# Modulation steps, context output rows and squares moved to other places in a diffusion layer's program

## The chip, the core and the metric

The kernel runs on one core of one Trainium2 chip. The metric is the device time of one execution in microseconds; the time before is the median of three runs. Inputs and outputs lie in the chip's memory (HBM).

## What is computed

The reference is one layer of a diffusion backbone: 1024 latent tokens and 256 context tokens, each 1024 wide, go through a half-step FFN, two token mixers side by side (a short gated convolution, and attention with grouped heads), a merge, and a second half-step FFN. All is float32.

```python
def rms_norm(x, g):
    y = x * lax.rsqrt(jnp.mean(x * x, axis=-1, keepdims=True) + EPS)
    return y * g
def modulate(h, shift, scale):
    return h * (1.0 + scale) + shift
def swiglu(h, w_in, w_out):            # w_in 1024 x 5632, w_out 2816 x 1024
    a, b = jnp.split(h @ w_in, 2, axis=-1)
    return (jax.nn.silu(a) * b) @ w_out
def short_conv(u, w): ...              # three taps along the tokens
def conv_branch(bg, cg, vc, conv_w):
    return bg * short_conv(cg * vc, conv_w)
def merge_branches(y_conv, o_attn, gate_logits, w_bc, w_ba, w_out):
    g_conv, g_attn = jnp.split(jax.nn.sigmoid(gate_logits), 2, axis=-1)
    return (g_conv * (y_conv @ w_bc) + g_attn * (o_attn @ w_ba)) @ w_out
```

Every sub-layer begins with such a norm and a modulation, and its result is added to the stream times a gate. The nine vectors of shift, scale and gate come from `silu(c) @ w_mod + b_mod` for the latent tokens and from `silu(c_ctx) @ w_mod + b_mod` for the context tokens; `w_mod` is 1024 x 9216.

## The kernel before

**Arithmetic.** A float32 product is made as three matmuls on rounded parts: `split` (line 187) casts a tile to its high part on ACT and subtracts it on DVE (now and then on POOL) for the low part; `mm3` takes high by high, high by low and low by high. A left operand's parts carry the names `wh` and `wl` (`wo` for output rows), a right operand's `r`, `rh`, `rl`.

**Winograd.** The large products over the 1024 latent tokens are taken as 2 x 2 blocks with seven products in place of eight (class `Winograd`). `lefts` loads weights (`raw`), forms sums of blocks on POOL (`s`), and hands out split left operands in a fixed order; `prefetch` draws them ahead; `product(i)` is 12 matmuls of 128 x 512 into one PSUM bank. Tiles `u`, `c`, `v`, `b`, `uc` hold the sums of the banks.

**The opening.** Tokens are transposed on PE, normed and split; meanwhile the first modulation vectors are made. `second_mod` (line 336) makes half a vector: DVE sums eight rows of `w_mod` times a scalar each (`macc<-rawm,silu_c`, one step each), then a split (`acch`, `accl`), two matmuls with a column of ones, a copy `mrow` on ACT, four transposes, and an addition into `modl`. It is a generator: `run(steps, n)` lets it advance by n steps, and where the program calls it decides where its instructions stand.

**The first FFN.** The loop over the 22 hidden blocks `j` makes each block's gate and value. From block `SIDE_FROM` = 12 on, the context tokens' product runs at the side of it, with the same weights (`side`, 48 matmuls of 128 x 256 and, at its end, `sa` and `hidc`, the hidden values of the context). After block 11 the twelve earlier blocks' sides are made by themselves, with the weights drawn again: this is called the context stage below. After every second block `context_out(j)` loads two rows of the output weights (`raw<-in_ffn_w_out_dram`), splits them (`wo`), and multiplies (`ps<-hidc,wo`, 48 matmuls), adding into `cacc`. `run(steps, STEPS[j])` advances the later modulation vectors (`later_mod`, line 262: loads of `rawm`, additions into `macc`, a product with ones, `mrow`, four small DMAs to `mcol`).

**The row products.** `row_products` (line 791) is the FFN's second matrix product, over the rows of the output weights and the hidden values read back from memory (`hid<-hd`), in the order i = 2, 1, 4, 6, 5, 7, 3 of the seven products, each in groups over pairs k of hidden blocks. `after1(i, k)` is called behind a group; it loads the stream `x` back, stores finished columns and makes their squares (`done`: `xd` stores, `sq` on ACT, `sq_acc` on DVE).

**The mixing.** `mix.start(norm1)` makes the first products of the next Winograd stage while the last right operands are normed; then a loop over eight blocks, `mixed`, makes the mixers' inputs, with `late_steps`, the last modulation vectors, run in it.

**What sets the order.** Each engine runs its instructions in its own order and waits on semaphores. Stretches of the program keep the order in which they are written; elsewhere a scheduler arranges it in the build. SP issues all DMAs of the main queue in order. Buffers come from rotating pools: 38 large tiles (`atile`), 11 tiles of 128 x 512 (`ttile`), three `raw` and four each of `wh` and `wl` for weights, and eight PSUM banks (five `ps`, two `pt`, one `po`). A load waits until the buffer that it writes is free.

All compute instructions are recorded at line 88, a wrapper round the engines, so the profile's groups are told apart by tile names.

```python
STEPS = (0, 4, 4, 4, 5, 5, 5, 5, 5, 5, 5, 14)
residual = {(2, 4): (C0, 0), (1, 6): (C0, 4), (4, 8): (C1, 0), (6, 4): (C1, 4)}
```

Of the kernel before, what the change touches and what calls it, by code (L numbers as in the profile page):

```python
# [10 lines left out]
F32R = mybir.dt.float32r  # L11
I32 = mybir.dt.int32
AF = mybir.ActivationFunctionType
ALU = mybir.AluOpType
# [27 lines left out]
STEPS = (0, 4, 4, 4, 5, 5, 5, 5, 5, 5, 5, 14)  # L42
# [7 lines left out]
def tile_dit_layer(  # L50
# [415 lines left out]
    class Winograd:  # L466
# [194 lines left out]
        def start(self, norm):  # L661

            for i in range(self.n_ahead):
# [3 lines left out]
                run(norm, 1)  # L667
# [123 lines left out]
    def row_products(w, rows, add, after=lambda i, k: None, halves=False):  # L791
# [113 lines left out]
        chain = [ps_t(), ps_t(), ps_o(), ps_s()]  # L905
        for i in (2, 1, 4, 6, 5, 7) + (() if halves else (3,)):
            ps = chain if i in (1, 6, 7) else [ps_s() for _ in range(4)]
# [99 lines left out]
    def left_operand(i, k):  # L1007
# [5 lines left out]
        else:  # L1013
            half1.shifted(h, c)
        half1.keep(1 + i, k, h)

# [39 lines left out]
    run(squares1, 1)  # L1056
    run(mod11, 3)
    run(start, 1)
    half1.prefetch(4, lo_engines=(pool, pool))
    run(squares1, 1)  # L1060
# [8 lines left out]
    run(mod11, 3)  # L1069
# [4 lines left out]
    run(mod11, 3)  # L1074
    run(start, 1)
    run(squares1)
    half1.prefetch(4)
    half1.rstd1 = token_rstd(ss1, 4)
    turned((4, 5))
    run(start, 1)  # L1080
    run(mod11)
    part_gain(gain1["l"], 0, "g1", "l", 4, 8)
    run(mod01, 9)
    half1.prefetch(4)
    turned((6, 7))
# [87 lines left out]
    def context_out(j):  # L1173

        ws = out_pieces(ffn1_w_out[0], (j - 1, j), spare=True)
        half1.prefetch(3)
        g = hid_c.pop(j // 2)
        for d in range(0, KD, 2):
            po = ps_s()
# [11 lines left out]

    for j in range(NH):
        half1.side = side(j) if j >= SIDE_FROM else None
        u, c = half1.next_first()
# [16 lines left out]
    for d in range(0, KD, 2):  # L1211
        t = ttile("cx")
        src = cxd[d // 4, :, (d % 4) * CT : (d % 4 + 2) * CT]
        sp.dma_start(out=t, in_=src)
        for e in range(2):
            te = t[:, e * CT : (e + 1) * CT]
            dve.scalar_tensor_tensor(
# [652 lines left out]
```

## Time and profile before

| | before |
|---|---|
| median of three runs | 2720.67 us (2720.63 to 2721.49) |
| the profiled execution | 2717.89 us, span 2716.1 us |
| mean granted clock of TensorE | 0.991 |
| PE busy in the span | 2647.6 us, 68.5 us idle |
| HBM read, written | 296.30 MB, 66.06 MB |

A row of the timeline gives start and length in microseconds, engine, line, operation, tiles written `<-` read, and in brackets the idle time of the engine ahead of it and what ended it. Rows of equal kind that follow one another are taken together (`x12`). A row of the windows gives the busy time of each engine in the stretch, the granted clock, the DMA engines' mean busy share and their rate. Times are counted from the span's start.

The opening lies at 0 to 110 us, the context stage at about 280 to 420, the row products of the first FFN from 693, the mixing's start at about 970.

### The profile page before, as it was taken

Reading aid. Unit: us, or ns where it says so; the run is one execution under the profiler, and the core shown is the slowest. Engines: PE = TensorE matmul, PEld = TensorE weight load, DVE = VectorE, ACT = ScalarE, POOL = GpSimd, SP = SyncE. Lnnn points to the kernel's source line nnn. Section 1 sums busy time; section 2 is a strip of 40 time slices with the busy share of each in tenths; the row PEclk is TensorE's granted clock in tenths of the full one; section 3 lists DMA queues with packets and bytes.
Section 4 is the critical chain, followed back from the end, with each engine's and each line's share of the span. In section 5 each row is a group of like instructions: output and inputs, shape, how many; then the busy total and the mean of one; then the engine's idle time right before and its main releaser. Section 6 shows DMA issues by size and latency. Waiting matters only on the chain.

```text
span 2716.1 us, 37388 instructions
## 1 busy us (share of the span) xinstructions
PE 2647.6 (97%) x13593; PEld 2236.8 (82%) x13593; DVE 2006.6 (74%) x3356; ACT 1167.2 (43%) x2317; POOL 532.1 (20%) x409
## 2 busy tenths in 40 slices
PE   7999899999999999999999999999999999999998
PEld 4788798888778877888999888877888888888888
DVE  5889666988787899888478576685548876667885
ACT  5633443333443542333245665674226333334443
POOL 1244001221010043333033111100000442330100
PEclk9999999999999999999999999999999999999998
DMA  7665553445984345433312321001533552227831
GB/s 264 212 195 170 166 168 100 147 129 179 324 206 105 113 151 186 135 118 120 109 32 87 97 82 43 28 32 47 175 105 124 179 163 93 86 89 283 183 86 63
DMA packets 369922, 364.85 MB, mean 134 GB/s; under 512 B 27831, under 2 KB 261449, under 8 KB 369737
## 3 DMA queue, kind: packets, MB, share of 16 engines
q1 hardware_dynamic: 360712, 345.17, 38.5%
q0 software_dynamic: 9024, 17.30, 4.0%
q8 instruction: 106, 1.74, 0.3%
q14 instruction: 80, 0.65, 0.1%
HBM read 296.30 MB, written 66.06 MB: 133 GB/s over the span
## 4 chain that ended last, share of the span: by engine, by line
PE 55%; DVE 3%; ACT 1%; issue 0%; DMA 0%; DVEq 0%; ACTq 0%
PE ps L88 45%; PE pt L88 5%; PE po L88 4%; DVE xb L88 0%; DVE ol L88 0%; ACT pts L88 0%; DVE pts L88 0%; DVE wl L88 0%; DVE x L88 0%; DVE r L88 0%; ACT pl L88 0%; DMA y<-yd 0%; ACT q L88 0%; ACT oh L88 0%; DVE t L88 0%
## 5 line engine op out<-in xcount | busy, mean ns | idle before, releaser
L88 PE MATMUL ps<-r,wl 128*128 128x512 f32 x5232 | 1208.9, 391 | 14.9 <-ACT wl L88 7.9
L88 PEld LDWEIGHTS ps<-r,wl 128*128 128x128 f32 x5232 | 979.8, 188 | 223.1 <-ACT wl L88 10.0
L88 ACT CAST wl<-raw 128x512 fp32r<-128x512 f32 x286 | 176.9, 620 | 291.2 <-PE ps L88 191.6
L88 POOL TENSOR_TENSOR s<-raw 128x512 f32<-128x512 f32 x64 | 95.5, 1492 | 1011.0 <-DMA raw<-in_ffn_w_in_dram 641.7
L88 ACT CAST wl<-s 128x512 fp32r<-128x512 f32 x256 | 158.0, 620 | 315.1 <-PE ps L88 233.4
L88 DVE TENSOR_TENSOR wl<-raw,wl 128x512 fp32r<-128x512 f32 x284 | 198.6, 700 | 80.8 <-ACT wl L88 77.0
L88 DVE TENSOR_TENSOR wl<-s,wl 128x512 fp32r<-128x512 f32 x256 | 230.3, 900 | 12.6 <-ACT wl L88 11.6
L88 POOL TENSOR_TENSOR s<-raw,s 128x512 f32<-128x512 f32 x64 | 107.3, 1677 | 355.2 <-DVE wl L88 347.3
L88 DVE SCALAR_TENSOR_TENSOR macc<-rawm,silu_c,macc 128x512 f32<-128x512 f32 x168 | 141.0, 855 | 8.5 <-DMA rawm<-in_w_mod_dram 7.4
L88 PE MATMUL ps<-wh,r 128*128 128x256 f32 x768 | 141.6, 285 | 0.0
L88 DVE TENSOR_TENSOR pts<-pt,pts 128x512 fp32r<-128x512 f32 x160 | 108.8, 687 | 39.3 <-ACT pts L88 38.3
L88 DVE TENSOR_REDUCE m<-ps 128x1 f32<-128x512 f32 (+1 forms) x192 | 110.9, 596 | 31.1 <-PE ps L88 30.3
L88 DVE TENSOR_TENSOR u<-u,ps 128x512 f32<-128x512 f32 x168 | 114.1, 679 | 23.2 <-PE ps L88 22.9
L88 ACT CAST pts<-pt 128x512 fp32r<-128x512 f32 x160 | 93.2, 593 | 88.6 <-PE pt L88 86.7
L88 PE MATMUL ps<-rh,wl 128*128 128x512 f32 x360 | 123.7, 395 | 3.9 <-ACT rh L88 3.9
L88 ACT CAST rh<-hid 128x512 fp32r<-128x512 f32 x132 | 81.0, 620 | 103.4 <-PE ps L88 86.3
L88 PEld LDWEIGHTS ps<-wh,r 128*128 128x128 f32 x768 | 120.6, 192 | 0.0
L88 ACT CAST wh<-raw 128x512 fp32r<-128x512 f32 (+1 forms) x88 | 69.4, 796 | 100.5 <-PE ps L88 73.0
L88 PE MATMUL po<-pts,vh 128*128 128x512 f32 x256 | 110.6, 438 | 1.5 <-ACT pts L88 1.5
L88 PE MATMUL ps<-wl,r 128*128 128x256 f32 x384 | 108.8, 283 | 0.0
L88 DVE TENSOR_TENSOR rl<-hid,rh 128x512 fp32r<-128x512 f32 x132 | 89.9, 686 | 23.8 <-ACT rh L88 11.4
L88 PE MATMUL ps<-kl,qs 128*128 128x512 f32 x384 | 105.3, 397 | 0.0
(295 smaller groups left out, 5082.0 us busy)
## 6 DMA issues: line engine op xcount, KB each, us to landing
raw<-in_ffn_w_in_dram SPq DMA_DIRECT2D x125, 512.0 KB
raw<-in_ffn_w_out_dram SPq DMA_DIRECT2D x72, 512.0 KB
rawm<-in_w_mod_dram SPq DMA_DIRECT2D x128, 256.0 KB
raw<-in_w_in_dram SPq DMA_DIRECT2D x61, 512.0 KB
hid<-hd SPq DMA_DIRECT2D x40, 512.0 KB
ws<-in_ffn_w_out_dram POOLq DMA_DIRECT2D x30, 512.0 KB, 6.6
ucd<-uc SPq DMA_DIRECT2D x22, 512.0 KB
hd<-c SPq DMA_DIRECT2D x38, 256.0 KB
```

Of the source, the lines that this page charges most:

```text
L88: inst = getattr(self.engine, name)(*args, **kw)
```

## The change

It has seven parts. In the opening, the steps of the two `second_mod` (`mod11` and `mod01`) and the token squares are called in other places, a few at a time; `mod11` begins with the first left operands. In the first FFN, `STEPS` becomes 2 at block 11 and 12 from block 12 on, and three steps are run at each of the context stage's twelve sides. `context_out` is cut into three: `context_rows` issues the row loads ahead of the pair's first side, `context_parts` splits them after it, and the product itself is made one pair late (`pending`, `context_last`); the last one, with the residual of the context, moves into the row products at (2, 0) and writes the `po` bank. `done(range(4), C0)` moves from (1, 11) to (4, 2). The four banks of the products 1, 6 and 7 are taken when i = 1 begins. `mix.start` advances its norm by 2, 1, 1, 1, 1, 3, ... in place of 1 each. The late modulation steps of the mixing are 5 + 4 + 4 in place of 13 at once.

```diff
-STEPS = (0, 4, 4, 4, 5, 5, 5, 5, 5, 5, 5, 14)
+STEPS = (0, 4, 4, 4, 5, 5, 5, 5, 5, 5, 5, 2, 12)
...
-                run(norm, 1)
+                run(norm, 2 if i == 0 else 1 if i < 5 else 3)
...
-        chain = [ps_t(), ps_t(), ps_o(), ps_s()]
+        chain = None
         for i in (2, 1, 4, 6, 5, 7) + (() if halves else (3,)):
+            if i == 1:
+                chain = [ps_t(), ps_t(), ps_o(), ps_s()]
...
-    def left_operand(i, k):
+    def left_operand(i, k, between=iter(())):
...
+        run(between, 1 - k % 2)
         half1.keep(1 + i, k, h)
+        run(between, 1 - k % 2)
...
+    mod11 = second_mod(1, 1, raws11)
     for k in range(4):
-        left_operand(0, k)
+        left_operand(0, k, mod11)
     start = half1.start_together()
-    mod11 = second_mod(1, 1, raws11)
     half1.prefetch(5, lo_engines=(pool, pool))
     for k, pt in banks.items():
         scaled(k, pt)
+    run(mod11, 2)
...
     turned((0, 1))
-    run(mod11, 3)
+    run(mod01, 3)
+    run(mod11, 1)
     run(start, 1)
     run(squares1, 1)
     half1.prefetch(4, lo_engines=(pool, pool))
     turned((2, 3))
-    run(mod11, 3)
+    run(mod11)
+    part_gain(gain1["l"], 0, "g1", "l", 4, 8)
+    run(mod01, 3)
...
+    turned((4, 5))
+    run(mod01, 3)
...
-    run(mod01, 9)
...
-    def context_out(j):
-
-        ws = out_pieces(ffn1_w_out[0], (j - 1, j), spare=True)
-        half1.prefetch(3)
+    def context_rows(j):
+        raws = []
+        for i in (j - 1, j):
+            t = atile("raw")
+            load(t[:], ffn1_w_out[0, i * P : (i + 1) * P, :])
+            raws.append(t)
+        return raws
+    def context_parts(j, raws):
+        ws = {}
+        for i, t in zip((j - 1, j), raws):
+            for half in range(2):
+                wt = wpool.tile([P, 2, 512], F32R, tag="wh", name=uniq("wo"), bufs=W_BUFS)
+                split(t[:, half * 512 : (half + 1) * 512], wt[:, 0], wt[:, 1])
+                ws[i, half] = wt
+        return ws
+    def context_out(j, ws, bank=ps_s):
         g = hid_c.pop(j // 2)
...
+    pending = []
+    def context_last(bank=ps_s):
+        if pending:
+            half1.prefetch(3)
+            context_out(*pending.pop(), bank)
     for j in range(NH):
         half1.side = side(j) if j >= SIDE_FROM else None
+        if j > SIDE_FROM and j % 2:
+            raws = context_rows(j)
...
             for i in range(SIDE_FROM):
+                if i % 2 == 0:
+                    raws = context_rows(i + 1)
                 do = side(i, ps_s)
                 for step in (1, 2, 0, 4):
                     do(step, half1.left())
-                if i % 2:
-                    context_out(i)
-        elif j >= SIDE_FROM and j % 2:
-            context_out(j)
+                run(steps, 3)
+                if i % 2 == 0:
+                    context_last()
+                    ws = context_parts(i + 1, raws)
+                else:
+                    pending.append((i, ws))
+        elif j > SIDE_FROM and j % 2:
+            pending.append((j, context_parts(j, raws)))
+        elif j >= SIDE_FROM:
+            context_last()
...
+    def context_residual():
+        context_last(ps_o)
+        for d in range(0, KD, 2):
...
+        if (i, k) == (2, 0):
+            context_residual()
+        if (i, k) == (4, 2):
+            done(range(4), C0)
         if k == NH // 2:
-            if i == 1:
-                done(range(4), C0)
-            elif i == 7:
+            if i == 7:
...
         if i > 1:
-            run(late_steps, 13)
+            run(late_steps, 5)
         for ch, bg, gc in mixed():
+            if i > 1:
+                run(late_steps, 4)
```

No engine has an instruction more or less; only places differ. Three of them follow in the built programs' order.

The first is DVE in the opening, before: `modl` is the addition that ends a modulation half, the eight `macc` rows sum the next half, `h` and `r` are the right operand that needs it.

```order
L88 TENSOR_TENSOR modl<-pt_510,bcol 128x4
L88 TENSOR_SCALAR gain_l<-modl 128x4
L88 TENSOR_TENSOR gain_l<-gain_l,cols 128x4
L88 TENSOR_SCALAR macc_518<-rawm_351,silu_c 128x512
L88 SCALAR_TENSOR_TENSOR macc_518<-rawm_351,silu_c,macc_518 128x512
L88 SCALAR_TENSOR_TENSOR macc_518<-rawm_353,silu_c,macc_518 128x512 x2
L88 SCALAR_TENSOR_TENSOR macc_518<-rawm_355,silu_c,macc_518 128x512 x2
L88 SCALAR_TENSOR_TENSOR macc_518<-rawm_357,silu_c,macc_518 128x512 x2
L88 TENSOR_TENSOR accl_528<-macc_518,acch_527 128x512
```

The same half in the changed program, on the same engine, stands as follows:

```order
L88 TENSOR_TENSOR accl_369<-macc_279,acch_368 128x512
L88 TENSOR_SCALAR macc_409<-rawm_358,silu_c 128x512
L88 SCALAR_TENSOR_TENSOR macc_409<-rawm_358,silu_c,macc_409 128x512
L88 SCALAR_TENSOR_TENSOR macc_409<-rawm_360,silu_c,macc_409 128x512
L88 TENSOR_TENSOR modl<-pt_451,bcol 128x4
L88 TENSOR_SCALAR gain_l<-modl 128x4
L88 TENSOR_TENSOR gain_l<-gain_l,cols 128x4
L88 SCALAR_TENSOR_TENSOR macc_409<-rawm_360,silu_c,macc_409 128x512
L88 SCALAR_TENSOR_TENSOR macc_409<-rawm_362,silu_c,macc_409 128x512 x2
L88 TENSOR_TENSOR wl_481<-raw_478,wl_481 128x512
L88 SCALAR_TENSOR_TENSOR macc_409<-rawm_364,silu_c,macc_409 128x512 x2
```

The second half's sums now begin ahead of the `modl` of the first, whose own sums lie among the lo parts of the first right operands.

The second place is SP's queue at the head of the context stage, before; `in_ffn_w_in` are loads of left weights, `in_ffn_w_out` the output rows of the first pair.

```order
L88 DMA raw_2667<-in_ffn_w_in_dram 128x8x128
L88 DMA raw_2807<-in_ffn_w_in_dram 128x8x128
L88 DMA raw_2809<-in_ffn_w_in_dram 128x8x128
L88 DMA raw_2878<-in_ffn_w_in_dram 128x8x128
L88 DMA raw_2719<-in_ffn_w_out_dram 128x1024
L88 DMA raw_2727<-in_ffn_w_out_dram 128x1024
```

In the changed program the first pair's rows stand in SP's queue so:

```order
L88 DMA raw_2482<-in_ffn_w_in_dram 128x8x128
L88 DMA raw_2550<-in_ffn_w_out_dram 128x1024
L88 DMA raw_2552<-in_ffn_w_out_dram 128x1024
L88 DMA rawm_2439<-in_w_mod_dram 128x512
L88 DMA raw_2570<-in_ffn_w_in_dram 128x8x128
```

The two rows are now ahead of modulation loads and of the left weights of the first sides. On PE, between the second pair's last side and the next side (`h1ch`, `h1cl`), before:

```order
L88 MATMUL ps_2948<-hidc_2856,wo_2934 128x256 x2
L88 MATMUL ps_2962<-hidc_2856,wo_2934 128x256 x2
L88 MATMUL ps_2976<-hidc_2856,wo_2937 128x256 x2
L88 MATMUL ps_2990<-hidc_2856,wo_2937 128x256 x2
L88 MATMUL ps_2948<-hidc_2856,wo_2934 128x256
L88 MATMUL ps_2962<-hidc_2856,wo_2934 128x256
L88 MATMUL ps_2976<-hidc_2856,wo_2937 128x256
L88 MATMUL ps_2990<-hidc_2856,wo_2937 128x256
L88 MATMUL ps_3004<-h1ch_1119,wl_2882 128x256
```

And on PE in the changed program, between two sides:

```order
L88 MATMUL ps_3023<-hidc_2796,wo_2864 128x256 x3
L88 MATMUL ps_3023<-hidc_2796,wo_2858 128x256 x3
L88 MATMUL ps_3023<-hidc_2796,wo_2864 128x256 x3
L88 MATMUL ps_3037<-hidc_2796,wo_2864 128x256 x3
L88 MATMUL ps_3037<-hidc_2796,wo_2858 128x256 x3
L88 MATMUL ps_3037<-hidc_2796,wo_2864 128x256 x3
L88 MATMUL ps_3051<-hidc_2796,wo_2867 128x256 x3
L88 MATMUL ps_3051<-hidc_2796,wo_2861 128x256 x3
L88 MATMUL ps_3051<-hidc_2796,wo_2867 128x256 x3
L88 MATMUL ps_3065<-hidc_2796,wo_2861 128x256 x3
L88 MATMUL ps_3065<-hidc_2796,wo_2867 128x256 x3
L88 MATMUL ps_3065<-hidc_2796,wo_2861 128x256 x3
```

Where 12 matmuls of the output product stood between two sides, 36 and more stand now, of the pair before.

The third place is DVE where the row products begin, before; `cacc` are the context's sums, `cx` its residual, `modl<-mcol` a late modulation vector, `rl` the lo parts of the rows:

```order
L88 TENSOR_TENSOR rl_6697<-hid_6636,rh_6696 128x512
L88 TENSOR_TENSOR rl_6718<-hid_6640,rh_6717 128x512
L88 TENSOR_TENSOR rl_6740<-hid_6640,rh_6739 128x512
L88 SCALAR_TENSOR_TENSOR cx_6614<-cacc_1123,gate_c,cx_6614 128x256 x2
L88 SCALAR_TENSOR_TENSOR cx_6619<-cacc_1123,gate_c,cx_6619 128x256 x2
L88 SCALAR_TENSOR_TENSOR cx_6624<-cacc_1124,gate_c,cx_6624 128x256 x2
L88 TENSOR_TENSOR rl_6761<-hid_6644,rh_6760 128x512
L88 TENSOR_TENSOR modl<-mcol_6532,bcol 128x4
```

And on DVE in the changed program, at the start of the row products:

```order
L88 TENSOR_TENSOR rl_6592<-hid_6560,rh_6591 128x512
L88 TENSOR_TENSOR cacc_1123<-cacc_1123,po_6632 128x512
L88 TENSOR_TENSOR u_6353<-u_6353,v_6413 128x512
L88 TENSOR_TENSOR rl_6617<-hid_6560,rh_6616 128x512
L88 TENSOR_TENSOR modl<-mcol_6536,bcol 128x4
L88 TENSOR_TENSOR cacc_1123<-cacc_1123,po_6646 128x512
L88 TENSOR_TENSOR wh_6613<-raw_6586,wh_6613 128x512
L88 SCALAR_TENSOR_TENSOR cx_6688<-cacc_1123,gate_c,cx_6688 128x256 x2
L88 TENSOR_TENSOR rl_6714<-hid_6564,rh_6713 128x512
L88 SCALAR_TENSOR_TENSOR cx_6693<-cacc_1123,gate_c,cx_6693 128x256 x2
```

The `modl` addition and the `cx` rows, which need DMAs, come ahead of the third `rl`, and the `cacc` additions are now in the row products.

More of the change, by code (lines that the diff above doesn't have):

```diff
@@ L1055, in tile_dit_layer @@
     squares1 = token_squares(t1, ss1)
-    run(squares1, 1)
     run(mod11, 3)
     run(start, 1)
+    run(squares1, 1)
     half1.prefetch(4, lo_engines=(pool, pool))
-    run(squares1, 1)
     def turned(ks):
@@ L1073, in tile_dit_layer @@
     turned((2, 3))
-    run(mod11, 3)
+    run(mod11)
+    part_gain(gain1["l"], 0, "g1", "l", 4, 8)
+    run(mod01, 3)
+    run(start, 1)
+    run(squares1, 1)
+    half1.prefetch(4)
+    turned((4, 5))
+    run(mod01, 3)
     run(start, 1)
@@ L1077, in tile_dit_layer @@
     half1.prefetch(4)
+    turned((6, 7))
+    run(mod01, 1)
     half1.rstd1 = token_rstd(ss1, 4)
[L1079 to L1082, printed above, removed]
-    run(mod01, 9)
-    half1.prefetch(4)
-    turned((6, 7))
     run(start, 1)
@@ L1171, in tile_dit_layer @@
     c_acc = Context("cacc")
-    def context_out(j):
-        ws = out_pieces(ffn1_w_out[0], (j - 1, j), spare=True)
-        half1.prefetch(3)
+    def context_rows(j):
[14 more added lines that the diff above has]
+    def context_out(j, ws, bank=ps_s):
         g = hid_c.pop(j // 2)
         for d in range(0, KD, 2):
-            po = ps_s()
+            po = bank()
             for e in range(2):
```

19 lines of the change are left out of this document (9 added, 10 removed).

## The prediction

> **What bounds the kernel now.** I read the page first, for the busy shares, the clock row and the costliest groups.
>
> ```profile
> span 2716.1 us, 37388 instructions
> PE 2647.6 (97%) x13593; PEld 2236.8 (82%) x13593; DVE 2006.6 (74%) x3356; ACT 1167.2 (43%) x2317; POOL 532.1 (20%) x409
> ...
> PEclk9999999999999999999999999999999999999998
> ...
> L88 DVE SCALAR_TENSOR_TENSOR macc<-rawm,silu_c,macc 128x512 f32<-128x512 f32 x168 | 141.0, 855 | 8.5 <-DMA rawm<-in_w_mod_dram 7.4
> ```
>
> The reader is to see that PE is busy for 2647.6 of 2716.1 us, so 68.5 us of idle time is all that a pure reordering can win, plus what the halved clock costs behind idle stretches. The change issues the same instructions on every engine (48 matmuls write another bank), so its whole price or gain is in PE's gaps. So I went next to the windows and the timeline of PE, at each place that the diff touches. First the windows (busy time of PE, PEld, DVE, ACT, POOL, then granted clock, DMA share and GB/s):
>
> ```profile
> 280.00:420.00 140.00, 122.71 (x936) 118.50 (x936) 90.28 (x144) 57.68 (x109) 9.14 (x6) 0.96 0.48 155
> 280.00:300.00 20.00, 14.12 (x104) 12.97 (x103) 19.56 (x32) 7.61 (x14) 0.00 (x0) 0.98 0.74 236
> 300.00:310.00 10.00, 5.80 (x28) 5.80 (x29) 4.84 (x10) 3.92 (x9) 0.00 (x0) 0.52 0.42 149
> 690.00:700.00 10.00, 8.46 (x38) 6.70 (x38) 5.69 (x10) 4.44 (x8) 0.00 (x0) 0.83 0.92 339
> 758.00:768.00 10.00, 6.79 (x23) 4.90 (x22) 9.90 (x17) 8.19 (x14) 1.21 (x1) 0.83 1.03 329
> 1074.00:1081.00 7.00, 3.99 (x10) 2.86 (x11) 6.79 (x12) 3.22 (x6) 2.73 (x2) 0.76 0.28 101
> 44.00:64.00 20.00, 14.09 (x74) 10.43 (x74) 14.06 (x32) 11.73 (x24) 1.31 (x1) 0.91 0.16 47
> ```
>
> The context stage, 280 to 420, alone holds 140 - 122.71 = 17.3 us of PE's idle time, a quarter of the whole. What ends those waits is the view of waits for PE in that window (total us, times, longest):
>
> ```profile
> PE ps L88 <- ACT wo L88: 10.1, 3, 9.0
> PE ps L88 <- DVE sa L88: 6.1, 5, 1.6
> PE ps L88 <- DVE wl L88: 1.1, 3, 0.6
> ```
>
> **The change part by part: the context stage.** The timelines of PE, ACT and SP's queue there:
>
> ```profile
> 304.20 2.08 PE L88 MATMUL ps<-hidc,wo 128*128 128x256 f32 x8 [8.98 <-ACT wo L88]
> 324.44 1.83 PE L88 MATMUL ps<-hidc,wo 128*128 128x256 f32 x12 [0.36 <-ACT wo L88]
> ```
> ```profile
> 303.53 2.37 ACT L88 CAST wo<-raw 128x512 fp32r<-128x512 f32 x4 [1.97 <-DMA raw<-in_ffn_w_out_dram]
> ```
> ```profile
> 290.86 7.96 SPq L88 DMA_DIRECT2D raw<-in_ffn_w_in_dram  x4
> 298.86 1.05 SPq L88 DMA_DIRECT2D raw<-in_ffn_w_out_dram  x2
> ```
>
> PE is still for 8.98 us because the cast of the first output rows starts at 303.53, when their DMA lands; and SP issues that DMA only at 298.86, behind four loads of weights for later left products that took it 7.96 us, each waiting for a buffer that DVE frees (DVE is busy for 19.56 of the 20 us before 300). In the changed order the two rows stand ahead of these loads and of the modulation rows, and their product is done one pair later, so three removals follow. The 8.98 us go. The halved clock behind them goes: 8 matmuls took 2.08 us at 304.20 where 12 take 1.83 at 324.44, and the window 300 to 310 shows a clock of 0.52; from 304.2 to near the end of that window, 5.4 us at half speed, 2.7 us are lost. And the 1.1 us left of the wo waits (10.1 - 9.0) go. The 6.1 us of waits for sa come where only 12 of the pair's matmuls (1.83 us) stand between one side's end and the next side, too few to cover ACT's and DVE's sa steps, which take 1.83 + 1.6 us by the longest wait; in the changed order 32 to 48 stand there (the 36 in the rows shown with the change are 3 x 1.83 = 5.5 us), so these go too, but for the 1.2 us at the stage's end. The 1.1 us for wl go, for the 14 modulation steps that crowd DVE at the stage's head become 2. So 8.98 + 2.7 + 1.1 + 6.1 + 1.1 = 20.0 us at most. Against it: by the order of the changed kernel 26 additions stand among the twelve sides' sa, where none stood (10 of them were in the crowd ahead, 16 are taken from later stages): 26 x 0.855 = 22.2 us of DVE by the mean of the macc group on the page, with 13 loads or more of 256 KB on SP's queue (13 make 3.4 MB, 24 GB/s on top of 155 over these 140 us, at a DMA share of 0.48). DVE has 140 - 90.28 = 49.7 us of room. I take 1.5 us of new short waits, with bounds 0 and 8 (six pairs at the longest sa wait here, 1.6, less 1.6): **18.5 us, between 12 and 20**.
>
> **The opening.** The timeline of PE, then of DVE, as the second modulation sums end:
>
> ```profile
> 53.90 2.99 PE L88 MATMUL ps<-r,wh 128*128 128x512 f32 x12
> 60.34 0.56 PE L88 MATMUL ps<-acch,ones_r 128*1 128x512 f32 x1 [3.44 <-ACT acch L88]
> ...
> 63.28 0.58 PE L88 MATMUL pt<-ident,mrow 1*128 1x1 f32 x4 [1.63 <-ACT mrow L88]
> 63.80 4.61 PE L88 MATMUL ps<-r,wh 128*128 128x512 f32 x12
> ```
> ```profile
> 54.16 5.48 DVE L88 SCALAR_TENSOR_TENSOR macc<-rawm,silu_c,macc 128x512 f32<-128x512 f32 x7
> ```
>
> PE loses 3.44 + 1.63 = 5.07 us, and 4.61 - 2.99 = 1.62 at the halved clock. The change puts the seven additions of 5.48 us among the earlier groups, DVE's lo parts among them. But the next left operands still need modl, and DVE's own work ahead of it stays the same, so the start moves by what DVE stood idle there, not by what PE lost: between 44 and 64 (the last window above) DVE is busy for 14.06 of 20 us, 5.9 idle, of which I count a little over half as usable, because each sum still runs through cast, lo part, two row products, mrow and transpose. Two new short stalls of PE on the earlier sum (about 1.0 and 1.5, the longer being the mrow wait above) are in it. **3.5 us, between 1 (only the transposes' wait shrinks) and 6 (5.07 + 1.62, less 0.7).** The first-half sums (mod01) move from one place to four in the groups behind it; DVE's total there stays, and the bounds hold them too.
>
> **The start of the row products.** The last pair's product moves into them:
>
> ```profile
> 693.12 1.20 PE L88 MATMUL ps<-rh,wl 128*128 128x512 f32 x4 [0.87 <-ACT rh L88]
> 694.98 0.56 PE L88 MATMUL ps<-rl,wl 128*128 128x512 f32 x1 [0.66 <-DVE rl L88]
> ```
> ```profile
> 683.69 9.09 SPq L88 DMA_DIRECT2D x<-xd  x8
> ```
> ```profile
> 670.51 0.16 DVE L88 TENSOR_TENSOR modl<-mcol,bcol 128x4 f32<-128x4 f32 x1 [3.75 <-DMA mcol<-mrow]
> ```
>
> What goes is 0.87 + 0.66, and 3.4 us at half clock (0.83 of ten), 1.7 lost: 3.2 us. What comes is DVE's modl and cx additions among the lo parts of the rows. These wait for DMAs that SP issues behind eight loads of x (9.09 us), and all that is behind them on DVE waits: rl, the lo parts of wh, and the cacc addition that frees the single bank of the product's next group. The four mcol copies are issued right behind; the one such wait in the trace is 3.75 us. Fewer modulation rows are fetched just ahead, so SP comes there some us earlier. Bounds of the new stall: 0, and 3.75 + 1.7 for its half clock + about 1.8 of cx, 7.2. I take 3.2, for a net of **0, between -4 and +3**.
>
> [...]
>
> **The squares and sums of the finished columns** move from (1, 11) to (4, 2):
>
> ```profile
> 762.51 1.22 PE L88 MATMUL ps<-rh,wl 128*128 128x512 f32 x4 [3.00 <-ACT rh L88]
> ```
> ```profile
> 760.13 1.82 ACT L88 ACTIVATE sq<-x 128x512 f32<-128x512 f32 x3
> 761.86 1.12 ACT L88 CAST rh<-hid 128x512 fp32r<-128x512 f32 x2
> ```
>
> Three squares (1.82 us, and a fourth at 758.7, as many times 0.6: 2.4) stand ahead of the rh cast that ended PE's 3.00 us; without them it can start near 759.6. The gap goes but for some 0.5, and half clock (0.83 over the ten us from 758: 3.4 us at half speed, 1.7 lost): 2.5 + 1.7, **4 us, between 2 and 5.** At (4, 2) ACT has the casts of later operands queued behind them, with PE's groups of 12 matmuls (2.99 us in the row at 53.90) as cover; uncovered it is the 2.4 us again, hence the lower end. The banks of the chain taken later free one wait near 731:
>
> ```profile
> 731.09 0.73 PE L88 MATMUL pt<-rh,wl 128*128 128x512 f32 x2 [1.57 <-DVE wl L88]
> ```
>
> That one ends at DVE, and its order shifts little: **1 us, between 0 and 3.**
>
> **The start of the mixing.** The three run(norm) counts:
>
> ```profile
> 972.63 1.22 PE L88 MATMUL ps<-r,wl 128*128 128x512 f32 x2 [3.50 <-ACT wl L88]
> ```
> ```profile
> 972.48 1.66 ACT L88 CAST r<-h 128x512 fp32r<-128x512 f32 x3
> ```
>
> At the mixing's start the only difference is that the cast and lo part of wl come behind all four r of that step, so by up to three casts (1.66) later, which lengthens the 3.50: **-1.3, between -3.4 (1.7 of half clock more) and 0.**
>
> **Late modulation steps** in the mixing, 13 at once become 5 + 4 + 4:
>
> ```profile
> 1076.98 2.42 PE L88 MATMUL ps<-r,wl 128*128 128x512 f32 x5 [4.35 <-ACT wl L88]
> ```
> ```profile
> 1067.03 5.61 DVE L88 SCALAR_TENSOR_TENSOR macc<-rawm,silu_c,macc 128x512 f32<-128x512 f32 x6 [1.54 <-DMA rawm<-in_w_mod_dram]
> 1072.68 0.62 ACT L88 CAST acch<-macc 128x512 fp32r<-128x512 f32 x1 [9.76 <-DVE macc L88]
> ```
>
> ACT stands still for 9.76 us in front of acch, because DVE waits for rawm and then adds for 5.61 us; PE's 4.35 us follow, and a clock of 0.76 over 1074 to 1081 (3.4 us at half, 1.7 lost). Spread, DVE's bank sums come between the additions: 4.35 + 1.7 less 0.5 is **5.5, between 2 (rawm as late as now) and 6.** The rest of the program keeps its order; the same instructions end it: 0, within 1.
>
> **Sum:** 18.5 + 3.5 + 0 + 4 + 1 - 1.3 + 5.5 = 31.2 us. The profiled run took 2717.89 us for a span of 2716.1; less 31.2 that is 2686.7. The median of the runs is 2720.67, 2.8 above the profiled run, so in the measure that counts I forecast **2689.5 us**.
>
> **The rivals.** *A new wait at the start of the row products.* For it speaks that SP's eight loads stand ahead of mcol and cx; against it that fewer rows are fetched just before. At its full 7.2 us with the mixing's start at -3.4 and DVE's additions costing 6 us in the context stage, it takes 4 + 2.1 + 4.5 = 10.6 off the gain: about 2700. *Only the gap for the rows goes.* If DVE is the limit in the context stage once PE stops waiting for rows, the sa waits turn into waits for wl, the opening gains 1, the late steps 2: 8.98 + 2.7 + 1.1 + 1 + 2 + 2 (squares) - 2.5 = 15, about 2705.5. *Slower: SP's queue held by the rows.* The rows now wait for a free slot of the large pool (all 38 are in use), and SP issues in order: if the slot is freed only by the product of the pair before, the left weights behind it are late, and PE starves at each of the six pairs. At the 8.98 us of the gap that just such a delay of loads made, six are 54 us, against a gain of 31: 2743; it decides from 31 / 6 = 5.2 us a pair. Against it: with a DMA share of 0.48 over the stage, the queue has time to be ahead of its users. *The change doesn't do what it says*: the rows of the two orders differ at each place named, so I give this no more than 1 in 100, at 2720.
>
> **How the numbers follow.** The forecast 0.60, the first rival 0.20, the second 0.10, slower 0.05, and 0.05 for a gain eaten to within 0.2% (5.4 us), about what a measurement of this kernel can tell from no change, the last rival in it. All good ends at once are 1.5 + 2.5 + 3 + 1 + 2 + 1.3 + 0.5 = 11.8 better, 2677.7; the other way, 8 in 10 and the doubt on the context stage want the first rival's 2700 and the second's 2705.5 inside: **2678 to 2706**. Faster 0.90, same 0.05, slower 0.05.
>
> **What would show it.** In the changed profile: no wait for wo over 1 us between 280 and 420, PE busy over 130 of 140 us there and a clock of 1.00; the acch wait in the opening under 1.5 us; no squares ahead of rh casts at the fourth column's groups; ACT's wait for acch near 1072 under 4 us. Wrong would be: PE waiting for ws or raw of left weights at the context pairs, DVE waiting over 3 us for mcol or cx near 690, a clock below 0.9 in a place where it was full.

## The result, and the profile after

The changed kernel takes 2694.62 us (median of 4 runs, 2691.16 to 2695.72), the kernel before 2720.98 (median of 4 runs beside it): a ratio of 0.9903 with a 95% interval of 0.989 to 0.9915, so 26 us or 1.0% faster. Forecast were 2689.5 us within 2678 to 2706. The profiled execution took 2694.38 us for a span of 2692.6, 23.5 less than the span before; the other 3 us are that the profiled execution of before was itself that much below its median.

The page, busy shares and clock row:

```profile
span 2692.6 us, 37398 instructions
PE 2642.8 (98%) x13593; PEld 2234.4 (83%) x13593; DVE 2009.5 (75%) x3356; ACT 1165.8 (43%) x2317; POOL 523.0 (19%) x409
...
PEclk9999999999999999999999999999999999999998
```

PE's idle time fell from 68.5 to 49.8 us, and its busy time by 4.8, as fewer matmuls ran at half clock (the mean granted clock is 0.994, before 0.991). To see where, I take the same matmul in both traces (the n-th of its kind) and compare their starts. What PE was ahead of before, in us, at points in the program's order, and the difference from point to point:

| up to | ahead | gained |
|---|---|---|
| end of the opening (before: 156 us) | -1.1 | -1.1 |
| before the context stage (280) | -2.1 | -1.0 |
| end of the first FFN's sides (680) | 16.4 | 18.4 |
| row products, first groups (709) | 19.3 | 2.9 |
| behind the waits at 725 and 731 | 23.0 | 3.7 |
| behind the wait at 759 | 28.2 | 5.2 |
| into product 6 (800) | 20.8 | -7.4 |
| rest of the row products (815) | 22.0 | 1.2 |
| mixing, before the late steps' wait (1072) | 22.3 | 0.3 |
| behind it (1083) | 28.8 | 6.5 |
| rest of the mixing (1197) | 26.8 | -2.0 |
| last matmul (2708) | 23.9 | -2.9 |

The windows, with the same columns as before: the context stage, the opening, and the end of product 4.

```profile
280.00:420.00 140.00, 137.87 (x1030) 130.75 (x1029) 117.60 (x198) 66.48 (x127) 11.75 (x8) 1.00 0.64 200
44.00:64.00 20.00, 19.09 (x102) 15.27 (x100) 11.86 (x29) 15.15 (x29) 3.09 (x2) 1.00 0.33 108
760.00:780.00 20.00, 15.41 (x57) 12.21 (x56) 11.32 (x17) 7.08 (x13) 4.60 (x4) 0.83 0.71 150
```

In the context stage 2.1 us of PE's idle time are left of 17.3, at a clock of 1.00 (0.96 before), while DVE works 117.6 us there in place of 90.3. What PE waits for in that window:

```profile
PE ps L88 <- DVE wl L88: 1.9, 2, 1.8
PE ps L88 <- DVE sa L88: 0.2, 1, 0.2
```

The waits for wo are gone, those for sa all but gone. PE's timeline in the opening, where the waits of 3.44 and 1.63 us stood, and further on, where new ones stand:

```profile
55.43 0.39 PE L88 MATMUL ps<-acch,ones_r 128*1 128x512 f32 x1 [0.57 <-ACT acch L88]
56.16 0.39 PE L88 MATMUL ps<-accl,ones_r 128*1 128x512 f32 x1 [0.34 <-DVE accl L88]
...
98.33 2.07 PE L88 MATMUL ps<-r,wl 128*128 128x512 f32 x4 [2.66 <-ACT uc L88]
...
121.11 0.30 PE L88 MATMUL pt<-ident,xtok 128*128 128x128 f32 x1 [2.77 <-DMA xtok<-in_ctx_dram]
```

Counted by place, PE is 2.4 us behind at 50 us of the kernel before and 5.9 ahead at 70. That gain is given back at 98 and 121, to other engines. SP's queue and DVE tell why:

```profile
112.62 1.01 SPq L88 DMA_DIRECT2D raw<-in_ffn_w_in_dram  x2
113.72 1.04 SPq L88 DMA_DIRECT2D ucd<-uc  x1
114.87 1.06 SPq L88 DMA_DIRECT2D xtok<-in_ctx_dram  x2
```
```profile
100.00:110.00 10.00, 10.00 (x41) 8.14 (x41) 10.00 (x15) 9.03 (x18) 4.56 (x3) 0.92 0.13 52
```

The context tokens are asked for only at 114.87, behind weights, as before (114.37); DVE is busy for all of the ten us from 100. PE, earlier, meets both.

At the end of product 4 stands the largest new wait, in PE's timeline, then ACT's and POOL's:

```profile
768.77 0.80 PE L88 MATMUL ps<-rl,wl 128*128 128x512 f32 x1 [4.59 <-DVE rl L88]
769.36 0.63 PE L88 MATMUL ps<-rh,wl 128*128 128x512 f32 x1
```
```profile
766.25 0.63 ACT L88 ACTIVATE ws<-ws 128x512 f32<-128x512 f32 x1 [7.78 <-DMA ws<-in_ffn_w_out_dram]
766.79 0.60 ACT L88 CAST wh<-ws 128x512 fp32r<-128x512 f32 x1
767.30 0.61 ACT L88 CAST rh<-hid 128x512 fp32r<-128x512 f32 x1
```
```profile
704.22 1.36 POOL L88 DMA_DIRECT2D ws<-in_ffn_w_out_dram  x1 [63.94 <-PE ps L88]
...
739.18 1.21 POOL L88 DMA_DIRECT2D ws<-in_ffn_w_out_dram  x1 [6.37 <-issue]
746.91 1.22 POOL L88 DMA_DIRECT2D ws<-in_ffn_w_out_dram  x1 [6.51 <-issue]
757.20 2.15 POOL L88 DMA_DIRECT2D ws<-in_ffn_w_out_dram  x2 [9.07 <-issue]
```

ACT stands 7.78 us before the negation of a weight sum (`ws`), and the rh cast that PE needs is queued behind it. The sums are made by loads that accumulate, that is, add what they bring to the tile that they write. They are issued on POOL's queue (`plus` in `row_products`), one every 7 to 11 us and the last two together. The first of eight is issued at 704.22, the last has landed when ACT goes on at 766.25: 62 us, while PE's products 1 and 4, which begin 2.2 us behind that first issue, take 60 (2 x 132 matmuls of 0.227 us).

The mixing's start and the late steps:

```profile
952.17 23.17 PE L88 MATMUL ps<-r,wl 128*128 128x512 f32 x95 [5.07 <-ACT wl L88]
...
1064.72 0.73 PE L88 MATMUL ps<-r,wl 128*128 128x512 f32 x2 [0.78 <-ACT wl L88]
1066.53 3.69 PE L88 MATMUL ps<-r,wl 128*128 128x512 f32 x15 [1.07 <-DVE wl L88]
```

5.07 us stand where 3.50 and 1.45 stood; of the 4.35 us near 1077, none is left at its place, and 1.85 us stand soon behind.

### The profile page after: what moved, and what is told of

Its sections match the earlier page's. It is cut to its first block, busy times and chain, and to the rows that moved or that the text cites. A ratio compares the mean times of both kernels' runs of the same rounds, so it can differ in the third digit from the quotient of the medians.

```text
span 2692.6 us, 37398 instructions
## 1 busy us (share of the span) xinstructions
PE 2642.8 (98%) x13593; PEld 2234.4 (83%) x13593; DVE 2009.5 (75%) x3356; ACT 1165.8 (43%) x2317; POOL 523.0 (19%) x409
## 4 chain that ended last, share of the span: by engine, by line
PE 84%; DVE 7%; DMA 4%; issue 3%; ACT 2%; SPq 1%; POOL 0%; DVEq 0%; ACTq 0%; POOLq 0%
PE ps L88 70%; PE po L88 7%; PE pt L88 7%; DMA rawm<-in_w_mod_dram 1%; DVE wl L88 1%; DMA raw<-in_ffn_w_in_dram 1%; DVE macc L88 1%; SPq L88 1%; DMA ws<-in_ffn_w_out_dram 1%; DVE r L88 0%; DVE xb L88 0%; ACT r L88 0%; DVE u L88 0%; DVE ol L88 0%; DVE y L88 0%
## 5 line engine op out<-in xcount | busy, mean ns | idle before, releaser
L88 DVE TENSOR_TENSOR wl<-s,wl 128x512 fp32r<-128x512 f32 x256 | 236.2, 924 | 8.5 <-ACT wl L88 6.8
```

Source lines behind the costliest of these rows:

```text
L88: inst = getattr(self.engine, name)(*args, **kw)
```

## The experiments

Each is the changed kernel with one edit, or with two of these edits together. On the chips of these runs the kernel before took 2722 to 2725 us (median), so the ratio to it is given, with its interval; place by place I compare the traces as above. Differences of under about 3 us between two runs can't be told by the times alone (the interval of the first ratio is 3.4 us to either side).

**The moved squares, undone and put later.** The edit of the first, then of the second:

```diff
-        if (i, k) == (4, 2):
-            done(range(4), C0)
         if k == NH // 2:
-            if i == 7:
+            if i == 1:
+                done(range(4), C0)
+            elif i == 7:
```
```diff
-        if (i, k) == (4, 2):
+        if (i, k) == (6, 2):
```

> The changed kernel with the stores and squares of the first four columns back at (1, 11). Supply theory (the rows of the second weight sums come by a chain of accumulating loads on POOL's queue, one after the other, and PE has overtaken it): the wait of about 3 us for rh near the end of product 1 comes back with its half clock (5 us), and PE, later by that, meets the chain at the end of product 4 with almost no wait, so the 4.59 us and the half clock there (7.4 us) go: 2692.5 us. Neighbour theory (the four stores, moved to just ahead of eight loads of x, stretch two of these accumulating loads): the same sum, 2692.5 us; the two theories part in the next run. A third, that the moved squares were a clear gain: 2699 us.

> The changed kernel with the same stores and squares later, at (6, 2), behind the loads of x. Supply theory: the wait at the end of product 4 stays, at least 4 us with its half clock: 2693 to 2696 us. Neighbour theory: the accumulating loads there take 7 to 8 us each in place of 10.3 and 9, the wait falls below 1.5 us and its half clock goes: 2686 to 2689 us.

Undone: 2697.6 us, ratio 0.9905 (0.989 to 0.992). The wait is back near the end of product 1,

```profile
741.17 2.08 PE L88 MATMUL ps<-rh,wl 128*128 128x512 f32 x4 [2.84 <-ACT rh L88]
```

and the one at the end of product 4 is gone; from point to point PE loses 6.1 us at the first and 7.4 less at the second, as both theories said, so that at 800 us of before the two kernels are half a us apart. The time is 5 us above their 2692.5 all the same: in this profile PE loses 6.2 us behind the late steps (1083 to 1197) where the changed kernel lost 2.0, or 3.7 in its second profile below, and why is open. Later: 2699.35 us, 0.9912 (0.9897 to 0.9927). There the wait at the end of product 4 is gone too, against the forecast of the supply theory; but the chain of loads took 59.5 us here (first issue 704.09, last landing 763.57), less than PE's 60, so the theory itself stands. Now product 6 pays:

```profile
778.90 0.74 PE L88 MATMUL pt<-rh,wl 128*128 128x512 f32 x2 [1.19 <-ACT rh L88]
784.65 0.79 PE L88 MATMUL pt<-rl,wl 128*128 128x512 f32 x1 [4.54 <-DVE rl L88]
```

7.1 us are lost there, half clock and all (from 785.24 to 788.23 the matmuls begin 0.43 us apart, then 0.24), so the time lies above both forecasts: the stores and squares cost as much in product 6.

**The opening, undone.** All calls of `mod11`, `mod01` and `squares1` as in the kernel before (the diff in the section on the change, reversed).

> The changed kernel with the opening of the kernel before. Given-back theory (DVE is full until 111 us in both, and the context tokens' loads stand behind it, so what PE gains at 60 us it waits for at 96 and 118): 2692 to 2695 us, and in the profile the waits of 2.66 and 2.77 us are gone while 3.4 us near 60 are back. Rival (the gain of 5.9 us at 64 us is real and the later waits are of other making): 2699 to 2701 us.

2690.99 us, ratio 0.9882 (0.9866 to 0.9897): not slower than the changed kernel. The waits of 3.44 and 1.63 us are back, the one at 98 is 2.08 us at 110, and none for xtok is left:

```profile
60.34 0.47 PE L88 MATMUL ps<-acch,ones_r 128*1 128x512 f32 x1 [3.44 <-ACT acch L88]
...
110.11 2.60 PE L88 MATMUL ps<-r,wl 128*128 128x512 f32 x10 [2.08 <-DVE wl L88]
```

At 156 us PE is 0.6 us ahead of the changed kernel: what the opening won it gave back in full. The rest of the 4 us of the medians lies at the end of product 4, where PE came within half a us of the same time as in the changed kernel and waited 0.61 us. There the first accumulating load was issued at 699.30 in place of 704.22:

```profile
699.30 1.36 POOL L88 DMA_DIRECT2D ws<-in_ffn_w_out_dram  x1 [59.46 <-DMA ws<-in_ffn_w_out_dram]
```

The tile that it adds to was asked for by SP and landed within 0.2 us of the same times in both (690.4 and 698.6; 690.6 and 698.8). What differs is what POOL waits for in the two built programs, told in the last section. So this part comes with the build and is not shown to be the opening's doing.

**The output rows, undone.** `context_out` as before, with its loads and splits, and with the last one and the residual ahead of the row products; `run(steps, 3)` at each side stays.

```diff
...
                 run(steps, 3)
-                if i % 2 == 0:
-                    context_last()
-                    ws = context_parts(i + 1, raws)
-                else:
-                    pending.append((i, ws))
+                if i % 2:
+                    context_out(i)
...
```

> The changed kernel with the context's output rows loaded, split and multiplied as before (same pair, loads behind the left weights, the last one ahead of the row products); the modulation steps stay as changed. Rows theory: the 9 us wait for the rows and the short sa waits come back, with the 3 us at the row products' start: 2709 to 2716 us. Steps theory (the crowd of 14 modulation steps made the loads late, and it is gone): only the sa waits (6 us) and part of the start come back: 2700 to 2704 us.

**The steps, undone.**

```diff
-STEPS = (0, 4, 4, 4, 5, 5, 5, 5, 5, 5, 5, 2, 12)
+STEPS = (0, 4, 4, 4, 5, 5, 5, 5, 5, 5, 5, 14)
...
-                run(steps, 3)
```

> The changed kernel with the modulation steps of the first FFN as before (14 at block 11, none among the twelve sides, 14 from block 12 on), the output rows ahead and a pair late as changed. Rows theory (the rows' place alone took the 9 us wait away): the context stage loses at most 3 us, the row products' start 0: 2694 to 2698 us. Steps theory (the crowd at block 11 was what delayed every load behind it, and the later stages' modulation loads stood in the way at the row products' start): 6 us or more in the context stage and 3 us at the start: 2702 to 2706 us.

Without the rows' part: 2700.51 us, ratio 0.9917 (0.9898 to 0.9935). Without the steps' part: 2701.8 us, 0.9922 (0.9908 to 0.9935). PE's waits in the stage (280 to 420), the first kernel's, then the second's:

```profile
PE ps L88 <- ACT wo L88: 5.4, 2, 4.8
PE ps L88 <- DVE wo L88: 1.0, 2, 0.8
PE ps L88 <- DVE sa L88: 0.5, 1, 0.5
```
```profile
PE ps L88 <- ACT hidc L88: 3.6, 1, 3.6
PE ps L88 <- DVE wl L88: 2.0, 2, 1.8
PE ps L88 <- ACT wl L88: 1.0, 1, 1.0
```

From 280 to 680 us of before, PE wins 18.4 us by both parts, 12.5 by the steps alone, 11.9 by the rows alone. So either part does more than half, and the two overlap: the steps theory was right that the crowd had delayed the loads (the longest wait for rows is 4.8 us without the rows' part, 8.98 before), but the rows add 5.9 us to it. The sa waits, 6.1 us before, go with either part: 0.5 us is left with the steps alone, none with the rows alone, where the pair's matmuls stand between the sides. The 2.9 us at the row products' start are won in both kernels, so each part is enough; the 3.7 us at 725 and 731 in neither, so they need both.

**The changed kernel once more, and the late steps undone.**

```diff
-            run(late_steps, 5)
+            run(late_steps, 13)
...
-            if i > 1:
-                run(late_steps, 4)
```

> The changed kernel itself, once more. Place theory: the wait of 4.59 us at the end of product 4 and its half clock belong to this order of instructions, and are there again, 4 us or more, with times within 2 us of 2694.6. Loads theory (when the first accumulating load lands decides, and that varies between executions; with the opening of before, PE came to the same place at the same time and waited only 0.61 us): the wait is another, anywhere from 0 to 5 us, and the times spread over 4 to 8 us.

> The changed kernel with the mixing's late modulation steps as before, 13 at once. By the prediction's term 5.5 us come back near 1072 (a wait of about 4.4 us and a half clock): 2699 to 2701 us; by the place-by-place count of the two traces, which shows 6.5 us won there and 2 us lost right behind, 4.5 us: 2698 to 2700 us. Rival (the gain there is only moved behind, to other waits of the mixing): 2693 to 2696 us.

Once more: 2695.98 us (2690.72 to 2700.0), ratio 0.9901 (0.9887 to 0.9914). The wait is there again, shorter, and here without a half clock (1.00 from 762 to 782; 3.6 us lost in place of 7.4):

```profile
770.94 0.50 PE L88 MATMUL ps<-rl,wl 128*128 128x512 f32 x1 [3.33 <-DVE rl L88]
```

The times of the five runs lie 9 us apart. So the place is the same and the length is not, as the loads theory has it, but not by its cause: the first load is issued 2.2 and 2.4 us ahead of product 1 in the two profiles, and the chain takes 62.0 and 60.8 us. It is the chain's length that varies, not its start.

Late steps at once: 2697.29 us, 0.9905 (0.9891 to 0.9918), 1.3 us more than the run beside it. By place, PE wins 0.5 us there from 1072 to 1197 in place of 4.5 (2.8 in the second profile of the changed kernel), with a wait of 3.29 us where the kernel before has 4.35: the term is worth 2 to 4 us by the traces, less than either forecast, and the times are too close to say more.

**The context tokens' loads early.**

```diff
     mod01 = second_mod(0, 1, raws01)
+    tx = fetch_tokens(CC)
...
-    tx = fetch_tokens(CC)
```

> The changed kernel with the two loads of context tokens issued at the modulation rows of the opening, ahead of the FFN's weights in SP's queue. Queue theory (at 118 us PE waits for these loads because SP issues them at 115 us behind weights that wait for POOL and DVE): the wait of 2.77 us and the half clock at 122 (1.7 us) go, 4 us less than the changed kernel: 2690 to 2691 us. Rival (DVE and POOL set the pace up to 125 us, so PE waits for something else there): within 1 us of the changed kernel.

2684.79 us, ratio 0.9861 (0.9848 to 0.9874), 11 us less than the changed kernel beside it. The wait for the loads became one of 0.93 us for DVE (1.80 us are left at 99 and 1.51 at 107, and the half clocks at 98 and 122 are gone: 26 matmuls from 98.99 take 6.20 us where the changed kernel has 7.77, and 20 from 120.09 take 4.80 where it has 3.23 for 8); by 156 us PE is 3.2 to 5.6 us ahead of the two profiles of the changed kernel. Of the rest, 6.1 us against the first profile and 2.4 against the second lie at the end of product 4, with a wait of 1.05 us. There the first accumulating load was issued 7.3 us ahead of product 1, as with the opening undone (6.7) and not as in the changed kernel (2.2), and for the same reason of the built program: this part of the gain is not shown to come from the tokens.

```profile
119.49 0.41 PE L88 MATMUL pt<-ident,xtok 128*128 128x128 f32 x2 [0.93 <-DVE xc L88]
```
```profile
760.73 0.50 PE L88 MATMUL ps<-rl,wl 128*128 128x512 f32 x1 [1.05 <-DVE rl L88]
```

**The second weight sums begun a pair earlier, and both.** In `sums`, where the number of pairs is n = 6:

```diff
-            if i == 1 and g >= 3 or i == 4 and g < n - 3:
-                k, m = groups[g - 3 if i == 1 else n - 3 + g]
+            if i == 1 and g >= 2 or i == 4 and g < 2:
+                k, m = groups[g - 2 if i == 1 else n - 2 + g]
```

> The changed kernel with the loads for the second weight sums, and the accumulating loads behind them, begun one pair of rows earlier in both row products. Supply theory (the chain of eight accumulating loads takes 60 to 62 us in the changed kernel's runs and PE's products 1 and 4 take 60; it starts only 2.2 us ahead of PE and so ends behind it): the chain ends 4 us or more earlier, the wait at the end of product 4 is under 0.7 us without a half clock, and the time is 4 to 7 us less: 2688 to 2692 us. Rival (the wait is for something else that stands there in ACT's order, such as the last row load): the wait stays over 3 us, and the time is within 2 us of the changed kernel's 2694 to 2696.

> The changed kernel with both the context tokens' loads early in the opening and the second weight sums begun a pair earlier. The kernel with early tokens took 2684.8 us and had a wait of 1.05 us left at the end of product 4. Supply theory: that one goes, no more: 2683 to 2685 us; the two gains overlap and don't add up. Rival (they are separate gains): 2678 to 2681 us.

Sums earlier: 2689.3 us, ratio 0.9878 (0.9863 to 0.9893). PE waits for nothing at the end of product 4; its window there is full, at full clock:

```profile
760.00:780.00 20.00, 20.00 (x90) 16.57 (x89) 13.97 (x21) 7.03 (x13) 4.60 (x4) 1.00 0.84 206
```

So that wait is the supply of weight sums. Both: 2682.77 us, ratio 0.9855 (0.9838 to 0.9871), with no wait left there; the gains overlap, as the supply theory said. With no wait at product 4 in either kernel, the early tokens are worth 6.5 us (2689.3 to 2682.77). It is the fastest kernel of the study, 12 us under the changed one, though not to be told from early tokens alone (2684.79).

**The banks, undone.**

```diff
-        chain = None
+        chain = [ps_t(), ps_t(), ps_o(), ps_s()]
...
-            if i == 1:
-                chain = [ps_t(), ps_t(), ps_o(), ps_s()]
```

> The changed kernel with the four banks of products 1, 6 and 7 taken ahead of product 2, as before. Banks theory (their late taking gave the 2.9 us at the start of the row products, and 3.7 us near 725, that came in every kernel so far with the late taking or only with both other parts): 3 us or more come back at the start, and the waits of about 1.5 us for wl: 2698 to 2702 us. Rival (the start is won by the fewer modulation loads and the moved product, and the banks change nothing that waits): within 1.5 us of the changed kernel.

2699.69 us, ratio 0.9916 (0.9902 to 0.9931). That is in the range of the banks theory, but not by its cause, so the theory falls: 2.9 us at the row products' start and 3.7 us near 725 are won as in the changed kernel. What it lost lies at the end of product 4:

```profile
772.36 0.80 PE L88 MATMUL ps<-rl,wl 128*128 128x512 f32 x1 [6.96 <-DVE rl L88]
```

Whether the banks made that wait longer, or the loads' landing, which differs between executions of one kernel too (62.0 and 60.8 us above), was not tried further.

**The squares alone, with the supply out of the way.** The edits of "sums earlier" and of "undone" squares together.

> The second weight sums begun a pair earlier, as in the run that took 2689.3 us, and the stores and squares of the first columns back at (1, 11). With the chain of accumulating loads out of the way the move of the squares stands alone. Covered-gain theory (the move is worth its 5 us, which product 4's wait hid in the changed kernel): the wait of 3 us near the end of product 1 and its half clock come back and are made up nowhere: 2693 to 2695 us. Rival (the move is worth nothing, since PE waits for loads in product 4 or 6 anyway): 2688 to 2691 us.

2695.42 us, ratio 0.9891 (0.9874 to 0.9907). The wait is back and not made up:

```profile
739.73 1.20 PE L88 MATMUL ps<-rh,wl 128*128 128x512 f32 x4 [3.00 <-ACT rh L88]
```

From 754 to 800 of before, PE gains 0.3 us here and 5.2 with the squares moved. So the move is worth 5 us by the traces (6 by the times), and the changed kernel doesn't get them, since PE meets the weight sums behind it.

## Why the prediction came out as it did

The sign and the range were right. By the profiles 23.9 us were won where the sum had 31.2. The medians miss the forecast by less, 5.1 us, because the changed kernel's profile lies only 0.2 us below its median, where 2.8 were allowed; that is luck. The signs of being right came: no wait for wo is left, PE is busy for 137.87 of 140 us in the context stage, it waits 0.57 us for acch in the opening, and ACT waits 3.22 us for acch in the mixing in place of 9.76.

- **The context stage** (18.5 forecast): 18.4 us up to the end of the sides. The sum was right; its working was so in part. The wait for the rows went as told. The sa waits went where matmuls of the pair before stand between the sides, as told, but fewer steps at the stage's head are enough for them too, which the prediction didn't see: it put them to the rows alone. It also counts their 6.1 us in full and says beside it that 1.2 stay.
- **The opening** (3.5, at least 1): -1.1. The step that failed: "the start moves by what DVE stood idle there". It did, by 5.9 us at 70 us. But the prediction ended there and didn't ask what PE meets next: DVE full until 111 us, and SP's loads of the context tokens at 115. Undoing the opening costs nothing; moving those loads gains. A clock below 0.9 in a place where it was full, one of the prediction's signs of being wrong, came here: 0.83 from 120 to 130 us, 1.00 before.
- **The start of the row products** (0): 2.9 us. The new wait for mcol and cx was over-priced at 3.2; the changed profile has 0.35 us there. Fewer modulation loads, or the moved product, each took the old waits away.
- **The squares** (4): 5.2 us won, just above the upper bound, and 7.4 lost at the end of product 4, at a clock of 0.83 from 760 to 780 where the kernel before had 1.00 from 780 to 800. The term's own mechanism was right, as the last run shows; the price "uncovered it is the 2.4 us again" looked at ACT's squares and not at POOL's accumulating loads, which no row of the prediction named. This is the step that failed most: its 7.4 us are as much as the sum missed by. That the other misses, from 4.6 too little at the opening to 2.9 too much at the row products' start, add up to nothing is luck. Some 4.7 us of the chain's lateness come with the built program (last section), which no row of the prediction shows.
- **Near 731** (1): 3.7 us, above the bound of 3; it needs both the rows and the steps, and not the banks to which it was put.
- **The mixing's start** (-1.3): near 0 (0.3 won before the late steps, with a wait of 5.07 for 4.95); the longer wait was followed by a shorter half clock (3.4 us, at 0.50 from 952 to 954 and 0.75 from 954 to 956; 6.8 before, at 0.50 from 972 to 978). In the second profile the half clock there lasts 6.8 us and 0.1 are lost, so this too is luck.
- **The late steps** (5.5): 6.5 won at the place and 2.0 lost behind it, 4.5 in one profile and 2.8 in the other; the waits moved in part.
- **The rest** (0, within 1): -2.9, of which 0.9 come at one wait before the attention (1.20 us for 0.28), 0.6 a little behind it, and the others at the end, where the half clock falls otherwise (0.50 from 2652 to 2658, and 1.00 from 2670 to 2678 of before). Two smaller rows of the table, -1.0 ahead of the context stage and 1.2 in the rest of the row products, were not forecast and are not explained.

Of the rivals, the wait for mcol and cx did not come, and SP's queue was not held by the rows. A new wait did take the place of old ones, but at the end of product 4 and through a queue that none of the rivals named.

## What to carry to other kernels

When waits are taken out of a chain, follow the engine to the next supply that comes in a chain, and compare both the lengths and the starts: 60 us of matmuls against 62 of loads that come one after the other, begun 2.2 us ahead, decided 7 of 31 us here. Where PE comes earlier and meets a load, look at when it is issued: moving two loads ahead gained 3.2 to 5.6 us by the end of the opening, where the spreading of all its steps gained nothing. Two edits that act on the same queue can overlap, as the steps and the rows did here (12.5 and 11.9 us alone, 18.4 together), so undo each alone before adding up their gains.

## What the runs showed of the hardware

The accumulating loads of 512 KB on POOL's queue follow one another: in the changed kernel three of them landed at 738.9, 746.6 and 756.9 us, and the next were issued at 739.18, 746.91 and 757.20, 0.3 us behind each. From issue to landing these took 7.3 to 10.0 us. Only the eighth, of 256 KB, was issued (757.93) before the one ahead of it had landed (764.9). The traces name no wait for most of these issues, so why POOL holds them back isn't shown.

Where the chain begins is a matter of the built program. The tile for the first accumulating load took the same 8.25 us from request to landing in both kernels (690.59 to 698.84 in the changed one, 690.39 to 698.64 with the old opening), at 407 GB/s and a DMA share of 1.05 from 690 to 700 in the changed one. By the trace's semaphores, POOL waits ahead of that first load for this one tile in the program with the old opening, and goes on 0.7 us behind its landing; in the changed kernel it waits for the next sum's tile too (landed at 700.8) and goes on 5.4 us behind the first landing. So it is in all fourteen traces: five programs with the one wait, the kernel before among them, issue 0.65 us behind the landing, nine with both 5.3 to 5.5 us. What POOL does in the 3.4 us between the second landing and the issue isn't shown. PE's wait at the end of product 4 goes with it. In the changed kernel twice, and with the late steps or the banks undone, all programs with both waits, PE waits 3.33 to 6.96 us there; with the old opening or early tokens, programs with the one, 0.61 and 1.05. (With the steps undone both waits are there and PE waits for nothing at that place, but it had lost 3.4 us to other waits at 717 and 721.)

No one length of wait goes with the half clock in these traces. In the first profile of the changed kernel the wait of 2.66 us at 98 went with 3.4 us at half clock (0.57 from 98 to 100, 0.58 from 100 to 102), and the 4.59 at 769 with 6.8 us (0.50 from 768 to 774); in its second, 3.33 us at 771 went with none, as the clock of this window shows:

```profile
762.00:782.00 20.00, 16.67 (x74) 13.48 (x73) 11.36 (x17) 7.07 (x13) 4.60 (x4) 1.00 0.76 152
```

What decides whether a wait brings the half clock, and for how long, these traces don't settle.
